# Streaming a 268 MB input past a dot product: 384-row tiles in four slots with an aligned load buffer, in place of 512-row tiles in three

## The chip, the cores and the metric

The kernel runs on one core of one Trainium2 chip. The metric is the time of one execution on the device in microseconds (us).

## The reference

```python
def setup_inputs():
    B, S, D = 8, 2048, 4096
    return {"x": np.random.randn(B, S, D).astype(np.float32),
            "w": np.random.randn(D, 1).astype(np.float32)}

def reference(x, w):
    proj = (x @ w).squeeze(-1)                 # one dot product per row of 4096
    cm = np.maximum.accumulate(proj, axis=1)   # running maximum over the 2048 positions
    is_record = (proj >= cm).astype(np.float32)
    return np.cumsum(is_record, axis=1).astype(np.float32)
```

The input `x` is 268.4 MB, and each element is used once.

## The kernel before

Each batch of `x` is cut along its positions into groups of 512, 512, 512 and 384, and a remainder of 128 positions. One load brings one batch's rows of one group: 128 partitions, four (or three) rows of 4096 float32 each, one after the other. VectorE (DVE) computes the dot product over columns 0 to 2815 (product and sum in one instruction, `w` broadcast in PSUM). GpSimd (POOL) multiplies the other 1280 columns, ScalarE (ACT) sums its products. At the end of a group TensorE turns the sums into rows of 8 batches, and DVE scans them. SyncE (SP) issues all large loads, in order.

```python
    RS = (4, 4, 4, 3)          # rows per partition in each group
    NS = 3                     # slots in the load buffer
    ...
    identity = sb([P, P], "identity")
    small = sb([P, 352], "small")
    masked = sb([P, 2 * P], "masked")
    fold = sb([P, 2 * B - H + Q], "fold")
    w2 = sb([P, W2C], "w2")
    xall = sb([P, NS * R * D], "xall")          # the load buffer: all slots
    ...
    def at(g, t):                                # the slot of tile t of group g
        return xbuf[(t if g < NL else t + NS - 1) % NS]

    def user_before(g, t):                       # whose tile must be done before this load
        if t >= NS:
            return t - NS, g + 1
        if g == NL:
            return B - NS + t, g
        return max(u for u in range(B) if u % NS == t), g
    ...                                          # SP: the loads
        for g in range(NG):
            r = RS[g]
            for t in range(B):
                i = SY.dma_start(
                    out=at(g, t)[:, : r * D],
                    in_=x[B - 1 - t, STARTS[g] : STARTS[g] + r * P, :].rearrange(
                        "(p r) d -> p (r d)", r=r
                    ),
                ).then_inc(xs[t], 16)
                u, n = user_before(g, t)
                if n:
                    i._wait_ge(*(free(u, n)))
    ...                                          # DVE: the dots of a group
        def group_dots(r, g=0):
            for t in range(B):
                b, xb = B - 1 - t, at(g, t)
                if r == R:
                    V.wait_ge(xs[t], 16).then_inc(go, 1)     # releases POOL at the landing
                for j in range(r):
                    i = dot(...)
                    if j == 0 and r < R:
                        i._wait_ge(xs[t], 16).then_inc(go, 1) # last group: after the first dot
                    elif j == 1:
                        i.then_inc(xs[t], -16)
                i.then_inc(fr[t], 1)
```

The last 128 positions come as tiles of 64 positions of two batches; their final batches are cut ever smaller, so that little work is left after the last byte. That part is the same in both kernels but for the slots it uses and 32 columns of one piece.

## Time and profile before

Before the change the median is 631.98 us (631.68 to 632.14, 3 runs).

| Reading, kernel before | Value |
|---|---|
| DMA engines busy | 9 tenths or more in 39 of 40 slices |
| bytes moved, mean rate | 268.55 MB, 426 GB/s |
| DVE, POOL, ACT busy | 65%, 59%, 29% |
| DVE waits for loads | 187.8 us in 32 waits |
| packets run | from 2.0 to 624.4 us of a span of 630.0 us |

The page of the kernel before, its 40 equal slices of the span: busy tenths of two engines, then of the DMA engines, and what they moved.

```profile
DVE  0755676546785557755579555676557966655897
POOL 0555676446765557755567555576555766666685
DMA  9999999999999999999999999999999999999995
GB/s 400 399 466 399 466 408 458 421 442 433 433 441 424 445 424 441 425 445 420 449 416 454 412 458 408 458 408 458 408 425 437 444 418 437 444 415 440 416 424 230
```

The DMA engines have work at nearly all times (the load queue fills 98.8% of the 16 engines' span), the compute engines do not (65% at most). The swing of the GB/s row, 399 to 466 in all slices but the last, goes with the size of the packets: with packets of 16 KiB, in an experiment below, 429 to 433 stand in all slices but the first and the last.

The waits of the kernel before: engine, line, what it waited for, us in total, times, longest.

```profile
DVE xall L127 <- DMA xall<-in_x_dram: 187.8, 32, 7.9
DVE cm L143 <- PE ps L319: 14.1, 3, 4.8
```

And the timeline of the kernel before, the first dot of successive tiles (start, us, engine, line; in brackets the wait before it): two tiles of 512 rows, then two of 384 in the last group.

```profile
42.40 3.09 DVE L127 CUSTOM_DVE_ANT_0 xall<-xall,w_v 128x2816 f32<-128x2816 f32 x1 [7.20 <-DMA xall<-in_x_dram]
61.74 3.09 DVE L127 CUSTOM_DVE_ANT_0 xall<-xall,w_v 128x2816 f32<-128x2816 f32 x1 [7.23 <-DMA xall<-in_x_dram]
...
570.92 3.09 DVE L127 CUSTOM_DVE_ANT_0 xall<-xall,w_v 128x2816 f32<-128x2816 f32 x1 [5.42 <-DMA xall<-in_x_dram]
585.45 3.09 DVE L127 CUSTOM_DVE_ANT_0 xall<-xall,w_v 128x2816 f32<-128x2816 f32 x1 [5.42 <-DMA xall<-in_x_dram]
```

A tile of 8.39 MB lands every 19.35 us, one of 6.29 MB every 14.53 us, and DVE waits for nearly each (at a group's end, where it has rows to scan, the next tile is already there). So the load stream sets the time: the bytes themselves, plus whatever each load or packet costs beside its bytes.

### The profile page before, as it was taken

The numbers are of one execution on the slowest core, as the hardware profiler recorded it, in microseconds if no ns is written. First come the engines' busy times: TensorE is split into PE (matmuls) and PEld (weight loads), VectorE is DVE, ScalarE is ACT, GpSimd is POOL, SyncE is SP. The second block draws the span as 40 slices with busy tenths as digits, with TensorE's granted clock in tenths as the row PEclk, the third lists the DMA queues.
The fourth block names the chain that finished last, engine by engine and source line by source line (L and its number), as shares of the span: only waits on it lengthen the run. The fifth ranks groups of instructions, "written<-read, shape, count | busy, mean of one in ns | idle before, by whom it ended". The sixth has DMA issues, their size and how long they took to land.

```text
span 630.0 us, 1182 instructions
## 1 busy us (share of the span) xinstructions
PE 31.7 (5%) x108; PEld 15.1 (2%) x108; DVE 406.9 (65%) x292; ACT 180.4 (29%) x273; POOL 370.1 (59%) x147
## 2 busy tenths in 40 slices
PE   8000000000010000000010000000002000000031
PEld 3000000000010000000010000000001000000010
DVE  0755676546785557755579555676557966655897
ACT  1222332123322233222233222332223232232353
POOL 0555676446765557755567555576555766666685
PEclk9999999999999999999996555555555555555555
DMA  9999999999999999999999999999999999999995
GB/s 400 399 466 399 466 408 458 421 442 433 433 441 424 445 424 441 425 445 420 449 416 454 412 458 408 458 408 458 408 425 437 444 418 437 444 415 440 416 424 230
DMA packets 6579, 268.55 MB, mean 426 GB/s; under 512 B 768, under 2 KB 1040, under 8 KB 1584
## 3 DMA queue, kind: packets, MB, share of 16 engines
q1 hardware_dynamic: 6560, 268.50, 98.8%
q10 hardware_dynamic: 16, 0.02, 0.0%
q14 instruction: 3, 0.02, 0.0%
HBM read 268.45 MB, written 0.07 MB: 426 GB/s over the span
## 4 chain that ended last, share of the span: by engine, by line
POOL 52%; issue 38%; DMA 6%; PE 2%; DVE 1%; SPq 0%; POOLq 0%; ACT 0%; ACTq 0%
POOL xall L287 52%; DMA xall<-in_x_dram 6%; PE w_v L231 2%; PE ps L231 0%; DVE xall L127 0%; SPq L199 0%; DMA w<-in_w_dram 0%; POOLq L290 0%; ACT w L242 0%; PE ps L373 0%; DVE cm_l L143 0%; DVE cnt_l L149 0%; DVE ps L146 0%; ACT xall L133 0%; DVE masked L365 0%
## 5 line engine op out<-in xcount | busy, mean ns | idle before, releaser
L127 DVE CUSTOM_DVE_ANT_0 xall<-xall,w_v 128x2816 f32<-128x2816 f32 (+3 forms) x133 | 388.4, 2974 | 187.8 <-DMA xall<-in_x_dram 187.8
L287 POOL TENSOR_TENSOR xall<-xall,w_sb 128x1280 f32<-128x1280 f32 x120 | 344.9, 2909 | 250.2 <-POOLq L290 250.2
L133 ACT ACTIVATE xall<-xall 128x1280 f32<-128x1280 f32 (+1 forms) x130 | 162.8, 1252 | 429.7 <-POOL xall L287 417.1
L319 PE MATMUL ps<-identity,small 128*8 128x128 f32 x60 | 13.1, 410 | 572.0 <-PEq L316 572.0
L133 ACT ACTIVATION_READ_ACCUMULATOR xall<-xall 128x1 f32 x130 | 24.2, 186 | 0.0
L343 POOL TENSOR_TENSOR xall<-xall,w_sb 128x1280 f32<-128x1280 f32 (+1 forms) x8 | 21.6, 2704 | 2.8 <-DMA xall<-in_x_dram 2.8
L319 PEld LDWEIGHTS ps<-identity,small 128*8 128x8 f32 x60 | 7.5, 128 | 578.8 <-issue 574.8
L143 DVE TENSOR_TENSOR_SCAN cm<-ps,cm,small 8x512 f32<-8x512 f32 (+1 forms) x5 | 6.1, 1216 | 14.1 <-PE ps L319 14.1
L231 PE MATMUL w_v<-w,identity 8*128 8x512 f32 x14 | 12.1, 1056 | 0.0
L127 DVE DVE_READ_ACCUMULATOR2_ANT small<- 128x1 f32 x133 | 10.8, 82 | 0.0
L253 DVE MEMSET ps<- 8x512 f32 x1 | 0.5, 485 | 15.5 <-ACT w L242 15.5
L149 DVE TENSOR_TENSOR_SCAN cnt<-ps,cnt,small 8x512 f32<-8x512 f32 (+1 forms) x5 | 6.1, 1217 | 0.2
L373 PE MATMUL ps<-fold,masked 128*8 128x64 f32 x32 | 4.6, 303 | 20.1 <-ACT masked L361 13.2
L231 PEld LDWEIGHTS w_v<-w,identity 8*128 8x128 f32 x14 | 4.6, 332 | 7.3 <-issue 7.3
L239 ACT COPY w_sb<-w_v 128x768 f32<-128x768 f32 x1 | 0.8, 799 | 11.4 <-PE w_v L231 11.4
L146 DVE TENSOR_TENSOR ps<-ps,cm 8x512 f32<-8x512 f32 (+1 forms) x5 | 3.3, 660 | 0.2
L373 PEld LDWEIGHTS ps<-fold,masked 128*8 128x8 f32 x32 | 2.5, 112 | 22.4 <-ACT masked L361 14.6
L361 ACT ACTIVATE masked<-fold,small 128x8 f32<-128x8 f32 x9 | 2.5, 297 | 0.2
L231 PE MATMUL ps<-w,identity 8*128 8x512 f32 x2 | 2.1, 1136 | 2.6 <-DMA w<-in_w_dram 2.6
L238 ACT ACT_TABLE_LOAD x1 | 1.3, 1283 | 2.7 <-DVE fold L249 2.7
L245 DVE TENSOR_REDUCE fold<-identity 128x2 f32<-128x128 f32 x1 | 0.3, 286 | 2.1 <-POOL cnt L224 2.1
L343 POOL TENSOR_TENSOR xall<-xall,w 128x352 f32<-128x352 f32 (+1 forms) x2 | 1.5, 766 | 0.2 <-DMA xall<-in_x_dram 0.2
(23 smaller groups left out, 7.0 us busy)
## 6 DMA issues: line engine op xcount, KB each, us to landing
xall<-in_x_dram SPq DMA_DIRECT2D x8, 6144.0 KB, 30.5
xall<-in_x_dram SPq DMA_DIRECT2D x6, 2048.0 KB, 39.5
xall<-in_x_dram SPq DMA_DIRECT2D x1, 1200.0 KB, 33.5
xall<-in_x_dram SPq DMA_DIRECT2D x1, 848.0 KB, 35.1
xall<-in_x_dram SPq DMA_DIRECT2D x1, 752.0 KB, 36.3
xall<-in_x_dram SPq DMA_DIRECT2D x1, 576.0 KB, 37.1
xall<-in_x_dram SPq DMA_DIRECT2D x24, 45.0
xall<-in_x_dram SPq DMA_DIRECT2D x1, 352.0 KB, 17.4
```

The source lines that it names most:

```text
L127: return V.tensor_tensor_reduce(out=xsl, in0=xsl, in1=wsl, scale=1.0, scalar=0.0, op0=ALU.mult, op1=ALU.add, accum_out=dst,)
L133: return A.activation(out=xsl, in_=xsl, func=ACTF.Copy, accum_out=dst)
L143: V.tensor_tensor_scan(out=cm_, data0=src, data1=low, initial=cm0, op0=ALU.max, op1=ALU.max,)._wait_ge(psr, base).then_inc(psr, 1)
L146: V.tensor_tensor(out=src, in0=src, in1=cm_, op=ALU.is_ge)._wait_ge(psr, base + 1).then_inc(psr, 1)
L149: V.tensor_tensor_scan(out=cnt_, data0=src, data1=low, initial=cnt0, op0=ALU.add, op1=ALU.max,)._wait_ge(psr, base + 2).then_inc(cs, 1)
L231: i = T.matmul(out=dst, lhsT=identity[:NW, k : k + 1].to_broadcast([NW, P]), rhs=w_row, start=True, stop=True,).then_inc(bw, 1)
L238: A.copy(out=w_sb[:, CV - VC :], in_=ps)._wait_ge(bw, 1).then_inc(wc, 1)
L287: i = G.tensor_mul(out=xl, in0=xl, in1=w_sb).then_inc(pl, 1)
L319: i = T.matmul(out=ps[:B, j : r * P : r], lhsT=l[:, j * B : (j + 1) * B], rhs=identity, start=k == 0, stop=k == 1,)
L343: G.tensor_mul(out=xl, in0=xl, in1=w_pool(*p))._wait_ge(xq[i], 16).then_inc(pl, 1)
L361: A.activation(out=e, in_=on, func=ACTF.Copy, scale=acc)._wait_ge(*wait).then_inc(ms, 1)
L373: return T.matmul(out=ps[:B, q : q + Q], lhsT=e, rhs=by_i, start=start, stop=bool(stop),)._wait_ge(*((mg, on_g) if pool else (ms, on_a)))
```

## The change

Its intent is smaller tiles with one load more in flight, programs of one loop per engine without a special last group, and a load buffer that starts at a multiple of 4096 bytes in each SBUF partition. The tensors `masked` and `fold` move behind the buffer and `w2` becomes 512 columns, which makes what stands ahead of the buffer a round number: in the built programs it starts at byte 21,952 before (192 past a multiple of 256) and at 20,480 after.

```diff
-    RS = (4, 4, 4, 3)
+    RS = (3, 3, 3, 3, 3)
-    NS = 3
+    NS = 4
-    W2, W2C = 1248, 544
+    W2, W2C = 1280, WC
     identity = sb([P, P], "identity")
     small = sb([P, 352], "small")
-    masked = sb([P, 2 * P], "masked")
-    fold = sb([P, 2 * B - H + Q], "fold")
     w2 = sb([P, W2C], "w2")
     xall = sb([P, NS * R * D], "xall")
 ...
     cnt = sb([B, N], "cnt")
+    masked = sb([P, 2 * P], "masked")
+    fold = sb([P, 2 * B - H + Q], "fold")
 ...
     def at(g, t):
-        return xbuf[(t if g < NL else t + NS - 1) % NS]
+        return xbuf[t % NS]
     def user_before(g, t):
-        (three cases)
+        return (t - NS, g + 1) if t >= NS else (t + B - NS, g)
 ...
             for t in range(B):
-                if r == R:
-                    V.wait_ge(xs[t], 16).then_inc(go, 1)
                 for j in range(r):
                     i = dot(...)
-                    if j == 0 and r < R:
+                    if j == 0:
                         i._wait_ge(xs[t], 16).then_inc(go, 1)
 ...
-        with V.Fori(0, NL):
+        with V.Fori(0, NG):
             group_scans()
             V.sem_inc(psr, -3)
             group_dots(R)
-        (the last group, written out)
 (the same on POOL, ACT and TensorE; the tail's tiles get slots t = 4, 5 and 6)
```

With one loop, POOL is always released after DVE's first dot of a tile (3 us after the landing), as only the last group did before.

More of the change, by code (lines that the diff above doesn't have):

```diff
@@ L41 @@
     NW = D // WC
-    RS = (4, 4, 4, 3)
+    RS = (3, 3, 3, 3, 3)
     R = RS[0]
-    NS = 3
+    NS = 4
     NG = len(RS)
-    NL = NG - 1
     N = R * P
@@ L62 @@
         (B - 1, 1440, 2592, (1792, 2592), (1440, 1792)),
-        (B - 1, 736, 1440, (736, 1248), (1248, 1440)),
+        (B - 1, 736, 1440, (736, 1280), (1280, 1440)),
         (B - 1, 352, 736, (352, 736), None),
@@ L153, in at @@
     def at(g, t):
-        return xbuf[(t if g < NL else t + NS - 1) % NS]
+        return xbuf[t % NS]
     def user_before(g, t):
-        if t >= NS:
-            return t - NS, g + 1
-        if g == NL:
-            return B - NS + t, g
-        return max(u for u in range(B) if u % NS == t), g
+        return (t - NS, g + 1) if t >= NS else (t + B - NS, g)
     def free(u, n):
@@ L189, in slot @@
         def slot(m):
-            if m < NS:
-                return None, xbuf[m][:, RS[-1] * D :]
-            u = B - NS if m < 2 * NS else B - NS + 1
-            return u, at(NL, u)[:, (m % NS) * D : (m % NS + 1) * D]
-        freed = {None}
+            u = B - NS + m // R
+            return u, at(NG, u)[:, m % R * D : (m % R + 1) * D]
+        freed = set()
         for i, (m, c0, c1, _, _) in enumerate(TILES):
@@ L278 @@
             group_dots(R)
-        group_scans()
-        V.sem_inc(psr, -3)
-        group_dots(RS[-1], NL)
         def group_products(r, g=0):
@@ L292 @@
         G.wait_ge(wc, 3)
-        with G.Fori(0, NL):
+        with G.Fori(0, NG):
             group_products(R)
-        group_products(RS[-1], NL)
         def group_sums(r, g=0):
@@ L307, in group_sums @@
             A.wait_ge(pd, 1).then_inc(pd, -1)
-        with A.Fori(0, NL):
+        with A.Fori(0, NG):
             group_sums(R)
-        group_sums(RS[-1], NL)
         def group_rows(r):
@@ L324, in group_rows @@
                         i.then_inc((pd, psr)[k], 1)
-        with T.Fori(0, NL):
+        with T.Fori(0, NG):
             group_rows(R)
-        group_rows(RS[-1])
         nv = npool = na = nm = on_a = on_g = 0
```

## The prediction

> **What bounds it now.** The load stream. The page's slices give DMA 9 everywhere but in the last, 426 GB/s over the span, and its queue table gives 98.8% of the 16 engines' span to the load queue. DVE is 65% busy, POOL 59%, ACT 29%. In the order of time one 512-row tile (8.39 MB) lands every 19.35 us; its work takes 12.1 us on DVE (4 dots of 3.01 us) and 11.5 us on POOL; DVE waits 187.8 us for loads. In the last group a 384-row tile (6.29 MB) lands every 14.54 us against 9.0 us on DVE.
>
> The trace's packets say how near the stream is to its limit: 65,536 B take 2420 ns (median), 49,152 B 1818 ns, 16,384 B 613 ns. The differences give 27.2 GB/s per engine, 435 GB/s for 16; what is left is a fixed 11 to 12 ns per packet. [...] All bytes at that rate are 617 us of the 622.4 us in which packets run (2.0 to 624.4 us). So 2% is not to be had: besides the bytes there are only the start (2.0 us), the tail (5.6 us after the last byte) and packet overhead.
>
> **What the change does.** Bytes are the same. Large loads go from 24 of 64 KiB per partition and 8 of 48 KiB to 40 of 48 KiB: per engine 424 packets instead of 360, an estimate of 64 x 12 ns = +0.8 us with the semaphore writes. Three slots of 19.35 us become four of 14.5 us; the queue holds two to three loads ahead in both. It never ran dry before (packets follow each other without gaps), so more slots gain nothing. The last group before already ran in the new form (POOL released after the first dot, 3 us later), at the same packet rate. At group ends (row matmuls about 2 us, scans about 3 us) DVE starts the next tile about 3 us late, with 5.5 us of slack per tile. The single loop only shortens the program. The tail has the same loads in the same order; its slots come free 14 us or more before the stream needs them; its last dots change by 32 columns (under 0.05 us).
>
> **The alignment** alone can move the bound. In the built programs the load buffer starts at byte 21,952 before (192 past a multiple of 256) and 20,480 after. [...] If not, net +0.8 us. I hold these about even, leaning to a partial saving.
>
> **Predicted:** 631.3 us, 628.2 to 633.4; faster by over 2%: 1%; within 2%: 97%; slower: 2%.
>
> **What would show it.** DMA 9 in all slices; 48 KiB packets of 1818 ns if alignment is worth nothing[...]; DVE waiting for loads at every tile; last byte to end 5.6 us.
>
> **What would make it wrong.** A slot freed too late (a digit below 9 mid-span, packets with gaps); 48 KiB loads running below the last group's rate when they are all there is[...].

## The result, and the profile after

The changed kernel takes 630.89 us (median of 4, 630.84 to 631.02) beside 631.85 us for the kernel before (median of 4, 631.68 to 632.14). The ratio is 0.9985, with a 95% interval of 0.9967 to 1.0002. A ratio here is the mean time of one kernel's runs over that of the other's of the same rounds, so not quite the ratio of the medians quoted. By that interval alone even the sign is not certain, though no run of the changed kernel was as slow as any run of the kernel before.

The page after, the same slices:

```profile
DVE  0756666659655555866666657556665966655897
POOL 0465556638666555556666639555555766666685
DMA  9999999999999999999999999999999999999996
GB/s 383 419 447 435 419 450 432 420 450 432 419 450 435 416 450 435 416 450 435 417 450 435 416 450 435 419 448 435 416 450 435 422 444 435 420 447 435 409 428 248
```

The waits after:

```profile
DVE xall L126 <- DMA xall<-in_x_dram: 171.0, 39, 5.5
DVE cm L142 <- PE ps L305: 29.1, 4, 7.3
```

The timeline after, first dots of two successive tiles in the last group:

```profile
569.81 3.09 DVE L126 CUSTOM_DVE_ANT_0 xall<-xall,w_v 128x2816 f32<-128x2816 f32 x1 [5.39 <-DMA xall<-in_x_dram]
584.31 3.09 DVE L126 CUSTOM_DVE_ANT_0 xall<-xall,w_v 128x2816 f32<-128x2816 f32 x1 [5.39 <-DMA xall<-in_x_dram]
```

DMA still bounds everything, and DVE still waits for nearly every tile. DVE's wait for TensorE at group ends grew from 4.8 to 7.3 us at the longest (POOL and ACT finish a group's last tile 3 us later), and it cost nothing: the tile after it was already there, and DVE waits for DMA again soon after. The tile pitch (the time from one tile's landing to the next) is what changed: 14.50 us where the kernel before needed 14.53 us for the same 384 rows. Over 40 tiles that would be 1.2 us, but the kernel before brings most rows in its larger tiles, at 19.35 us each (14.51 us per 384 rows), so the pitch alone does not give the difference of the two kernels.

The packet records show it more sharply. This table is worked out from the records of the load queue in each trace (packets of 512 B and more in this and later tables; "stream" is from the first load packet's start to the last one's end):

| | before | after |
|---|---|---|
| 64 KiB packets, median | 2420 ns | none |
| 48 KiB packets, median / mean | 1818 / 1819.9 ns | 1815 / 1817.3 ns |
| 16 KiB packets, median / mean | 613 / 614.8 ns | 611 / 612.0 ns |
| load packets per engine | 360 | 424 |
| stream | 622.45 us | 621.23 us |
| last byte to end of span | 5.57 us | 5.55 us |

The stream became 1.2 us shorter although it carries 64 packets more per engine, and the span with it (630.0 to 628.8 us). Nothing happened at its two ends.

### The profile page after: what moved, and what is told of

The parts are those of the page before. It is cut to its first block, busy times and chain, and to the rows that moved or that the text cites. A ratio compares the mean times of both kernels' runs of the same rounds, so it can differ in the third digit from the quotient of the medians.

```text
span 628.8 us, 1211 instructions
## 1 busy us (share of the span) xinstructions
PE 32.2 (5%) x108; PEld 14.9 (2%) x108; DVE 407.1 (65%) x295; ACT 180.1 (29%) x273; POOL 369.5 (59%) x147
## 4 chain that ended last, share of the span: by engine, by line
POOL 52%; issue 38%; DMA 6%; PE 2%; DVE 1%; SPq 0%; POOLq 0%; ACT 0%; ACTq 0%
POOL xall L275 52%; DMA xall<-in_x_dram 6%; PE w_v L224 2%; DVE xall L126 0%; PE ps L224 0%; DMA w<-in_w_dram 0%; SPq L192 0%; POOLq L278 0%; ACT w L235 0%; PE ps L358 0%; DVE cm_l L142 0%; DVE cnt_l L148 0%; DVE ps L145 0%; ACT xall L132 0%; POOLq L281 0%
## 5 line engine op out<-in xcount | busy, mean ns | idle before, releaser
L142 DVE TENSOR_TENSOR_SCAN cm<-ps,cm,small 8x384 f32<-8x384 f32 x6 | 6.0, 1003 | 29.1 <-PE ps L305 29.1
L148 DVE TENSOR_TENSOR_SCAN cnt<-ps,cnt,small 8x384 f32<-8x384 f32 x6 | 6.0, 1004 | 0.2
L145 DVE TENSOR_TENSOR ps<-ps,cm 8x384 f32<-8x384 f32 x6 | 3.3, 554 | 0.2
L358 PEld LDWEIGHTS ps<-fold,masked 128*8 128x8 f32 x32 | 2.5, 112 | 22.2 <-ACT masked L346 14.5
```

Of the source, the lines that this page charges most:

```text
L142: V.tensor_tensor_scan(out=cm_, data0=src, data1=low, initial=cm0, op0=ALU.max, op1=ALU.max,)._wait_ge(psr, base).then_inc(psr, 1)
L145: V.tensor_tensor(out=src, in0=src, in1=cm_, op=ALU.is_ge)._wait_ge(psr, base + 1).then_inc(psr, 1)
L148: V.tensor_tensor_scan(out=cnt_, data0=src, data1=low, initial=cnt0, op0=ALU.add, op1=ALU.max,)._wait_ge(psr, base + 2).then_inc(cs, 1)
L358: return T.matmul(out=ps[:B, q : q + Q], lhsT=e, rhs=by_i, start=start, stop=bool(stop),)._wait_ge(*((mg, on_g) if pool else (ms, on_a)))
```

## The experiments

Two theories stood against each other. Theory 1: the aligned start makes every packet cheaper, and the smaller tiles give some of that back. Theory 2: the smaller tiles and the fourth slot gain, and the address is nothing. Seven kernels ran, one of them in both sets, each five times in rounds with the kernel before, and all were correct. In the first set the kernel before took 631.70 us (median of 9), in the second 631.69 us.

### The kernel before with an aligned buffer

Only the order of the small tensors changes, so that the buffer starts at byte 20,480; tiles, slots and loops are those of before.

```diff
     masked = sb([P, 2 * P], "masked")
-    fold = sb([P, 2 * B - H + Q], "fold")
-    w2 = sb([P, W2C], "w2")
+    cm_l, cnt_l = (sb([B, P], n) for n in ("cm_l", "cnt_l"))
     xall = sb([P, NS * R * D], "xall")
+    w2 = sb([P, W2C], "w2")
+    fold = sb([P, 2 * B - H + Q], "fold")
```

> The kernel before with 512-row tiles and three slots, only the small tensors reordered so that the load buffer starts at byte 20,480. Theory 1 (an aligned start is cheaper to write): 64 KiB packets fall from a median of 2420 ns to about 2417, 48 KiB ones from 1818 to 1815, 16 KiB ones from 613 to 611, and their spread shrinks; with fewer packets than the change the time is about 630.3 us, 0.5 us below the changed kernel. Theory 2 (the gain comes from smaller tiles and four slots, the address is nothing): packets and time stay as before, 631.8 us.

Measured: 630.40 us (630.16 to 630.90), ratio 0.9978 (0.9964 to 0.9992). 64 KiB packets have a median of 2418 ns, 48 KiB ones 1815, 16 KiB ones 611, and all 768 of the last kind took exactly that. Three successive first dots in its last group, against 14.53 us between both pairs before:

```profile
555.76 3.09 DVE L127 CUSTOM_DVE_ANT_0 xall<-xall,w_v 128x2816 f32<-128x2816 f32 x1 [5.47 <-DMA xall<-in_x_dram]
570.26 3.09 DVE L127 CUSTOM_DVE_ANT_0 xall<-xall,w_v 128x2816 f32<-128x2816 f32 x1 [5.39 <-DMA xall<-in_x_dram]
584.78 3.09 DVE L127 CUSTOM_DVE_ANT_0 xall<-xall,w_v 128x2816 f32<-128x2816 f32 x1 [5.41 <-DMA xall<-in_x_dram]
```

The same kernel ran again in the second set, beside a changed kernel shifted by 256 B (below):

> The kernel before with an aligned load buffer, once more, beside the others on one chip: 630.2 to 630.9 us, at or just under the changed kernel, since it sends 64 packets per engine fewer at about 5 ns each (0.3 us).

Measured: 630.48 us (630.24 to 630.71), ratio 0.9980 (0.9966 to 0.9993). Alignment alone gives 1.2 to 1.3 us, more than the whole change. Theory 2 falls. This kernel, before with three lines moved, also beats both: the aligned 384-row kernel in the same set took 630.92 to 631.11 us, without overlap.

### The changed kernel with the old address

```diff
     w2 = sb([P, W2C], "w2")
+    pad = sb([P, 368], "pad")          # 1472 B, never used
     xall = sb([P, NS * R * D], "xall")
```

> The changed kernel with an unused 1472 B ahead of the load buffer, so that it starts at byte 21,952 as in the kernel before. Theory 1: 48 KiB packets back at 1818 ns, tail packets uneven again, time about 632.3 us, above both kernels (more packets, none of the saving). Theory 2: stays at 630.9 us with 1815 ns.

Measured: 632.52 us (632.36 to 632.63), ratio 1.0013 (0.9999 to 1.0027), with 48 KiB packets at 1818 ns. Its timeline, first dots in the last group:

```profile
571.01 3.09 DVE L127 CUSTOM_DVE_ANT_0 xall<-xall,w_v 128x2816 f32<-128x2816 f32 x1 [5.42 <-DMA xall<-in_x_dram]
585.54 3.09 DVE L127 CUSTOM_DVE_ANT_0 xall<-xall,w_v 128x2816 f32<-128x2816 f32 x1 [5.42 <-DMA xall<-in_x_dram]
```

The pitch is back at 14.53 us. Together the four corners are (medians; before and the two experiments from the first set, the changed kernel from its own comparison):

| | start 192 past a multiple of 256 | start at a multiple of 4096 |
|---|---|---|
| 512-row tiles, 3 slots | 631.70 us (before) | 630.40 us |
| 384-row tiles, 4 slots | 632.52 us | 630.89 us (after) |

Read across, alignment is worth 1.3 to 1.6 us. Read down, the smaller tiles, with the slots and loops that come with them, cost 0.5 to 0.8 us. The change is the sum of a gain and a smaller loss. (Moving the buffer also moves what is allocated behind it. In the kernel before with an aligned buffer, the sizes added up in order, which give the two recorded addresses, put `w_sb`, `cm` and `cnt` 192 B past a multiple of 256, as before, and the packets are short all the same (48 KiB in 1815 ns): so it is the buffer.)

### Which multiple counts: shifts of 256 and 128 bytes

The same edit with pads of 256 B and 128 B.

> The changed kernel with the load buffer 256 B later (20,736: a multiple of 256, not of 512 or 4096). [...] 48 KiB packets stay at 1815 ns with no spread in the small tail packets, time as the changed kernel (630.9 us); if 4096 is needed, 1818 ns and about 632.5 us as with the shift of 1472 B.

Measured: 631.01 us (630.92 to 631.11), 48 KiB packets at 1815 ns.

> The changed kernel with the load buffer 128 B later (20,608: a multiple of 128, not of 256). [...] 1818 ns, about 632.5 us. If 128 B is enough: 1815 ns, 630.9 us. (1472 is a multiple of 64, so 64 B alone is already known not to be enough.)

Measured: 632.28 us (632.21 to 632.57), 48 KiB packets at 1818 ns. So a multiple of 256 is enough, 4096 is more than is needed, and 128 is not enough.

Is it the start in SBUF alone? Some of the small tail pieces speak for it. Two of them start at column 0 of their row, so at the buffer's own offset (mean packet times from the trace records):

| Bytes per packet | offset 0 (after) | offset 128 (shift 128) | offset 192 (shift 1472) |
|---|---|---|---|
| 6784 | 258.0 ns | 259.3 ns | 263.3 ns |
| 1408 | 60.0 ns | 60.0 ns | 62.6 ns |

For these two an offset of 192 costs 5.3 and 2.6 ns, one of 128 only 1.3 and 0.0 ns; for a packet of 48 KiB both take the median from 1815 to 1818 ns. But two facts of the same traces speak against a price that the start in SBUF alone sets:

- The other five tail pieces start at columns that lie 128 B past a multiple of 256. With the shift of 128 they start at a multiple of 256, and yet they got no faster: those of 4608, 2816 and 1536 B went from 178.0 to 178.4 ns, 112.0 to 112.0 and 65.0 to 65.05, the 9600 B ones from 361.0 ns to 362.6. In the kernels with an aligned buffer, such a piece starts equally far past a multiple of 256 in its row of `x` and in SBUF, and every one of a size takes the same time (in the changed kernel all 128 packets of 4608 B took 178 ns, and all 128 of 9600 B took 361).
- Both shifted kernels began at the aligned pace. Their second to fourth loads have 48 KiB packets with a median of 1815 ns (means 1815.1 to 1816.1, beside 1815.0 to 1815.8 in the changed kernel) and tiles 14.50 us apart; from the seventh load on the medians are 1818 ns and more, and the tiles 14.53 us apart.

So what counts may be the offset in SBUF against that of the source and not the SBUF address alone (all large loads here read whole rows of 16 KiB), and the 3 ns came only with the later loads. No run moved the source, and the mechanism stays open.

### Three slots in place of four

```diff
-    NS = 4
+    NS = 3
 ...
-        return (t - NS, g + 1) if t >= NS else (t + B - NS, g)
+        if t >= NS:
+            return t - NS, g + 1
+        return max(u for u in range(B) if u % NS == t), g
```

> The changed kernel with three slots of 384 rows instead of four. Theory 1: the stream never runs dry with three either, time within 0.2 us of the changed kernel (630.9 us) and packets at 1815 ns. Theory 2: part of the gain goes, about 631.5 us or more, with gaps between packets.

Measured: 644.57 us (644.17 to 645.28), ratio 1.0205 (1.0191 to 1.0219). The expectation of theory 1 missed by 13.7 us. The packets still have a median of 1815 ns, but the stream runs dry. Around the first group's end, the windows view of this run (the columns are the window in us, its length, busy us and count of PE, PEld, DVE, ACT and POOL, granted clock, DMA share, GB/s):

```profile
100.00:118.00 18.00, 0.00 (x0) 0.00 (x0) 9.40 (x8) 5.96 (x9) 11.59 (x5) 1.00 1.00 434
118.00:121.00 3.00, 0.00 (x0) 0.00 (x0) 0.84 (x1) 0.86 (x2) 0.00 (x0) 1.00 0.92 281
121.00:134.00 13.00, 0.20 (x2) 0.16 (x3) 8.28 (x6) 4.09 (x6) 8.62 (x3) 1.00 0.96 416
134.00:137.00 3.00, 2.51 (x12) 1.28 (x10) 0.45 (x1) 0.00 (x0) 0.00 (x0) 1.00 0.76 311
```

And the timeline of the same run says why:

```profile
105.67 3.09 DVE L126 CUSTOM_DVE_ANT_0 xall<-xall,w_v 128x2816 f32<-128x2816 f32 x1 [5.39 <-DMA xall<-in_x_dram]
...
108.85 8.62 POOL L277 TENSOR_TENSOR xall<-xall,w_sb 128x1280 f32<-128x1280 f32 x3 [5.88 <-POOLq L280]
...
118.67 0.19 ACT L132 ACTIVATION_READ_ACCUMULATOR xall<-xall 128x1 f32 x1
118.89 15.39 SPq L168 DMA_DIRECT2D xall<-in_x_dram  x3
120.16 3.09 DVE L126 CUSTOM_DVE_ANT_0 xall<-xall,w_v 128x2816 f32<-128x2816 f32 x1 [5.38 <-DMA xall<-in_x_dram]
```

The seventh tile landed at 105.65 us; POOL started only after DVE's first dot, at 108.85; ACT let go of the slot at 118.86, 13.2 us after the landing. With slots counted `t % 3` in groups of eight, the next group's first tile takes the slot of the seventh, and the loads behind it wait in SP's order. So at a group's end just one load (the eighth tile, landing at 120.14) is in flight while the next one waits for a slot, and it is issued 1.25 us before that landing. The first packets of a load came 1.0 us after its issue at the start of the kernel, so a lead of 1.25 us is hardly enough: the rate falls to 281 GB/s. A second dip, to 311 GB/s, follows where the next load waits for TensorE to release the eighth tile's slot (14.2 us). The next group's tiles land about 118 to 120 us after the last group's, in place of the 116 us of eight tiles at 14.50 us; over four group ends that is the 13 us.

### Three slots, with POOL released at the landing

```diff
             b, xb = B - 1 - t, at(g, t)
+            V.wait_ge(xs[t], 16).then_inc(go, 1)
             for j in range(r):
                 i = dot(...)
-                if j == 0:
-                    i._wait_ge(xs[t], 16).then_inc(go, 1)
-                elif j == 1:
+                if j == 1:
                     i.then_inc(xs[t], -16)
```

> The three-slot form of the changed kernel, with POOL released at the landing of a tile as in the first groups of the kernel before, instead of after the first dot. In the three-slot run a slot came free 13.2 us after its tile landed and the next load at a group's end was issued only 1.25 us before the running one ended. Theory 1 (the loss is late slot release): a slot comes free about 10.2 us after landing, the lead grows to about 4 us, the gaps vanish and the time is 630.9 to 631.3 us. Theory 2 (three slots of this size are too few in any case): stays near 644 us.

Measured: 631.08 us (630.90 to 631.42). The windows view of this run, the same stretches:

```profile
100.00:118.00 18.00, 0.00 (x0) 0.00 (x0) 9.40 (x8) 5.23 (x8) 8.63 (x3) 1.00 1.01 437
118.00:121.00 3.00, 0.00 (x0) 0.00 (x0) 0.77 (x1) 0.00 (x0) 0.82 (x1) 1.00 0.99 412
121.00:134.00 13.00, 2.72 (x12) 1.50 (x12) 8.94 (x7) 4.09 (x6) 7.81 (x3) 1.00 0.99 428
134.00:137.00 3.00, 0.00 (x0) 0.00 (x0) 2.93 (x4) 0.00 (x0) 1.75 (x1) 0.96 0.95 410
```

The slot of the seventh tile is now free 10.2 us after its landing (105.50 to 115.65 us), the next load is issued 4.4 us ahead of the eighth tile's landing, and 412 GB/s stand where 281 did. What remains at 134 us is a brief low that costs nothing measurable: the groups are 116 us apart again. So three slots of this size are enough if they come free early; the change lets them go late, and its fourth slot is what makes that harmless. It is a need that the change itself creates, not a gain.

### Three times the packets

```diff
+                for j in range(r):
                     i = SY.dma_start(
-                        out=at(g, t)[:, : r * D],
+                        out=at(g, t)[:, j * D : (j + 1) * D],
                         in_=(the rows of this tile; here row j of each partition),
                     ).then_inc(xs[t], 16)
 ...
-                        i._wait_ge(xs[t], 16).then_inc(go, 1)
+                        i._wait_ge(xs[t], 16 * r).then_inc(go, 1)
```

> The changed kernel with each large load issued as three loads of one row per partition: 16 KiB packets, 640 more per engine, and 80 more semaphore writes. With a fixed cost of 8.5 to 9 ns per packet and 9 ns per semaphore write (theory 1, which counts packets): +5.4 to +5.8 us and +0.7 us, time about 637.2 us. If the packet count costs nothing, 630.9 us.

Measured: 634.36 us (634.25 to 634.54), ratio 1.0042 (1.0028 to 1.0056). That is +3.5 us over the changed kernel, little more than half of what was expected, though the packets took just the 611 ns that the expectation rested on. The DMA view of this run (the same rows as on the page):

```profile
DMA  8999999999999999999999999999999999999995
GB/s 356 431 431 431 433 432 431 432 432 431 431 431 432 431 431 431 431 432 431 432 430 431 431 431 431 431 433 431 431 431 432 431 431 431 432 431 431 430 429 241
```

The stream is still gapless, at a steady 431 GB/s. The miss lies in how the records were read. Added up, the packets and semaphore writes of an engine do come to 628.2 us against 621.7 us (+6.5 us, as expected), but the stream lasted 625.0 us against 621.2 us (+3.8 us). The records overlap. From 190 to 220 us in this trace, a packet most often starts 607 ns after the packet 16 places before it (619 of 771), though each is recorded as 611 ns; in the changed kernel's trace the repeat is 1812 ns (172 of 245; 1811 in 51), though each is recorded as 1815. From the two repeats, (1812 - 607) ns for 32,768 B is 27.2 GB/s, and 607 ns less 16,384 B at that rate leaves 4.5 ns per packet. Where an engine writes a semaphore between two packets, the repeat is 6 ns longer (613 and 1818 ns). 640 packets at 4.5 ns and 80 semaphore writes at 6 ns are 2.9 + 0.5 us of the 3.5 us measured.

## Why the prediction was right or wrong

The total was right: 631.3 us with 628.2 to 633.4 was said, within 2% at 97%, and 630.9 us came. Point by point:

- **The load stream bounds both kernels: right.** DMA 9 in all slices but the last, DVE waiting for loads 39 times, a tail of 5.57 and 5.55 us. The differences of the packet times give 27.2 GB/s per engine (435 GB/s for 16), and at that rate the bytes alone are 617 of the 622.45 us of the stream before. This is why no part of the change could be worth 2%.
- **"64 x 12 ns = +0.8 us": right in size, not in its unit.** The corners give +0.5 to +0.8 us for the smaller tiles. But the fixed cost of an aligned packet is about 4.5 ns, not 12: 3 to 4 ns of the 12 are overlap in the records (611 and 1815 ns recorded, 607 and 1812 ns from start to start) and about 3 to 4 are misalignment. 64 packets at 4.5 ns and 8 semaphore writes at 6 ns are 0.34 us. With aligned buffers the difference measured is 0.5 us; the rest was not found, and it is within the spread of the runs. (In steady state the traces show 19.319 us for an aligned 512-row tile, which is 14.489 us for 384 rows, beside 14.500 us: 0.43 us over 40 tiles. Their whole streams do not show it, since among the first seven tiles of the kernels with 512 rows a few took 0.2 to 0.7 us longer; why is open.)
- **The alignment: right that it alone moves the bound; its size was only estimated.** The prediction held a saving and no gain (+0.8 us net) about even and leaned to a partial saving. How large the saving would be was the author's estimate; nothing in the trace before showed it. The gain exists, and it is 1.3 to 1.6 us; 48 KiB packets were to stay at 1818 ns if alignment was worth nothing, and took 1815. By the time that is (631.70 - 630.40) us / 360 packets = 3.6 ns per packet, or (632.52 - 630.89) us / 424 = 3.8 ns, and for the start 128 B past a multiple of 256 (632.28 - 631.01) us / 424 = 3.0 ns. Of the starts tried, those 0 and 256 B past a multiple of 4096 gave 1815 ns, those 128 and 192 B past a multiple of 256 gave 1818. Why a shifted start costs what it does was not shown.
- **Net: a gain of 1.3 to 1.6 us less 0.5 to 0.8 us is about the 0.96 us measured.** The prediction reached a value near it (631.3 us, 630.9 measured) by weighing the author's estimate of a saving against the +0.8 us; the size of that saving was not shown, and that the value came so near is luck. The range that held rests on the bound, not on this term.
- **"It never ran dry before, so more slots gain nothing": true as said, incomplete in its reason.** With tiles of 14.5 us and POOL released after the first dot, a slot is held for 13.2 us, and three slots cost 13.7 us. The prediction saw the late release and costed it only against DVE's slack, not against the lead with which the next load is issued. In the changed kernel the fourth slot covers it, so the total did not suffer; the experiment's own expectation, which copied this step, missed.
- **Single loop, 32 columns more: right, worth nothing that shows.** The span's two ends did not change.

## What to carry to other kernels

When gapless loads bound a kernel, compare the bytes at the per-engine rate (27.2 GB/s here) with the length of the stream before anything else: here 617 of 622 us were bytes, and every idea about slots, loops and tile sizes had the other 5 us to share. In such a kernel start the load buffer at a multiple of 256 bytes (here 1815 in place of 1818 ns per 48 KiB packet; the large loads read whole rows of 16 KiB, and sources that start elsewhere were not tried), which costs nothing but the order of the small tensors, and keep the packets long; the version with both, the old tiles with the aligned start, was the fastest of all at 630.4 us. And when tiles shrink, set the time from a tile's landing to its slot's release against the time of the loads still in flight, at group ends above all: here a release 3 us later cost 13 us with three slots (644.57 beside 631.08 us) and nothing with four (630.89 us).
